# Prefetched residual, a pinned first stage and later cache copies in a two-layer hybrid decoder

## The chip, the cores and the metric

The kernel runs on 1 core of one Trainium2 chip. The metric is device time in microseconds (us), the median over runs. PE is TensorE, DVE VectorE, ACT ScalarE, POOL GpSimd; SP, ACT and POOL also issue DMAs, each in a queue of its own.

## The reference

Two decoder layers, in fp32, for 1024 prompt tokens and 8 sample tokens that share the weights. Each sub-layer is wrapped in two RMS norms: h = h + post_norm(f(pre_norm(h))).

```
ap = rms_norm(hp, norm_mix_pre[l]);  a_s = rms_norm(hs, norm_mix_pre[l])
layer 0: q, k, v, r, z = split(x @ w_in)        # 512, 512, 1024, 1024, 16 columns
         log_a = log_sigmoid(z @ w_gate2 + b_gate) / 16
         o, s  = gated linear recurrence over q, k, v, log_a     # 4 heads
         m     = (rms_norm(o, g_head) * silu(r)) @ w_out
layer 1: sliding-window attention (window 128, sinks, partial rotary), samples on a cache
h = h + rms_norm(m, norm_mix_post[l])
h = h + rms_norm(relu(rms_norm(h, norm_ffn_pre[l]) @ w_up[l])**2 @ w_down[l], norm_ffn_post[l])
```

The outputs are both hidden states, the recurrence's states, and the last keys and values. For the samples the key and value cache goes out shifted by one position: 127 old rows per sample are copied, one new row is added.

## The kernel before, in words

**Groups and products.** Group A holds tokens 0 to 511 and the 8 samples (520 columns, in chunks of 256 and 264), group B tokens 512 to 1023. Activations lie with the features on the partitions, in 8 pieces (k) of 128. Each fp32 operand is split into a high part (an ACT copy to fp32r) and a low part (a DVE subtraction), and a product is three matmuls: high by high, low by high, high by low (`mms`, lines 225, 227, 229). A weight tile of 512 rows by 128 columns is fetched on SP's queue (`fetch_w`, line 195, three buffers) and split by ACT and DVE (`split_w`, lines 201 and 202, four buffers). The 16 gate columns z have their own `fetch_z`, `split_z` (lines 236, 241, 242) and `mms_z` (line 260).

**Order.** A scheduler may reorder instructions on each engine; those handed to `tc.keep_in_program_order` keep their order among themselves. Products stand in a list (`pending`), and work beside them is written as generators that `tick` advances: each step yields an estimate of its time, and each product gives credit.

**First stage.** `load_x` reads A's tokens in blocks of 128 (`fetch`, line 457) and the gain vector, spread over 128 partitions (line 496). For each block `stats` squares it with a row sum on ACT (line 465), makes the mean on DVE (468) and the -0.5 power on POOL (469); `scale` multiplies two halves by it and by the gain on DVE (477); `turn` transposes on PE (489) and splits into xh and xl (304, 305). Blocks go in the order 0, 1, 2, 3, samples; SP fetches block 0, gain, blocks 1 and 2, wz and two weight tiles, block 3, samples. The splits of wz and of the weights of the first tile of r come behind the squares of block 2, those of the second tile behind block 3. `gla_part1` then runs for A, chunk by chunk, z and the first two tiles of r, and calls `load_params` (lines 131 to 143: eleven small loads on POOL, line 117, with nine DVE operations behind them). `load_gate` (six loads on POOL, line 444, then lines 445 and 446) comes behind A's blocks. The samples' part of the cache copies (line 1098, DRAM to DRAM, on POOL) stands in the second layer's code; nothing holds it there.

**Residual.** `post_norm` scales piece k by gain and rstd (line 371) and calls `residual(k)`. After the first layer's mixer that is `from_input`: ACT's queue fetches the piece's columns of x (line 387, three buffers shared with the norms), PE turns four blocks (391), DVE adds (393); for A a 4 KB load of the samples' columns (396), a transpose (398) and an addition (399) follow, for each piece. The next norm (`pre_norm`, through `rstd_gen`) squares each piece on ACT (317, 320), adds the squares on DVE (321), and makes the new xh and xl (361, 304, 305). This runs beside group B's output projection; A's FFN comes next on PE.

Of the kernel before, what the change touches and what calls it, by code (L numbers as in the profile page):

```python
# [12 lines left out]
F32 = mybir.dt.float32  # L13
# [55 lines left out]
def tile_hybrid_gla_swa_decoder(  # L69
# [50 lines left out]
    def halved(t, n, name):  # L120

        o = const.tile([P, n], F32, name=name)
        nc.vector.tensor_scalar_mul(o, t, -0.5)
        return o
# [6 lines left out]
    def load_params():  # L131
        nonlocal bg_t, gh_t, bqkv_t, bo_t, bq8
        bg_t = load_cols(b_gate[0], GH, "bg_t")
        gh_t = halved(load_cols(g_head[0], 2, "gh_r"), 2, "gh_t")
# [7 lines left out]
        bq8 = const.tile([P, 8], F32, name="bq8")  # L142
        nc.vector.tensor_scalar_mul(bq8, bqkv_t[:, 0:8], 0.125)
# [297 lines left out]
    def load_gate():  # L441
# [3 lines left out]
        nc.scalar.copy(out=wg3, in_=wgs)  # L445
        nc.vector.tensor_tensor(out=wg3[64:96], in0=wgs[64:96], in1=r(wg3[64:96]), op=ALU.subtract)

    def load_x(g, box, tiles, early=None):
# [3 lines left out]
        blocks = list(range(g.nb)) + ([g.nb] if g.ns else [])  # L452

        def fetch(n):
            rows = P if n < g.nb else g.ns
            src = x_prompt[0, (g.b0 + n) * P:(g.b0 + n + 1) * P, :] if n < g.nb else x_sample[:, 0, :]
            nc.sync.dma_start(out=tiles[n][:rows], in_=src)

        def stats(n):
# [5 lines left out]
            sq = nc.scalar.activation(out=jk[:rows], in_=t, func=AF.Square, accum_out=ss[:rows, 0:1])  # L465
            if g.i == 0 and n > 0:
                tc.keep_in_program_order(sq)
            nc.vector.tensor_scalar(out=ms, in0=ss[:rows, 0:1], scalar1=1.0 / D, scalar2=EPS, op0=ALU.mult, op1=ALU.add)
            nc.gpsimd.tensor_tensor(out=y, in0=ms, in1=half[:rows], op=ALU.pow)
            return y  # L470

        def scale(n, y, pin=False):
            rows = P if n < g.nb else g.ns
            t = tiles[n][:rows]
            for hf in range(2):
                c = slice(hf * 512, hf * 512 + 512)
                v = nc.vector.scalar_tensor_tensor(out=t[:, c], in0=t[:, c], scalar=y, in1=gbc[:rows, c],
                                                   op0=ALU.mult, op1=ALU.mult)
                if pin:
                    tc.keep_in_program_order(v)  # L480

        def turn(n):
            rows = P if n < g.nb else g.ns
            t = tiles[n][:rows]
            for hf in range(2):
# [12 lines left out]
        if not ahead:  # L498
            for i in range(len(blocks)):
                fetch(blocks[i])  # L500
                scale(blocks[i], stats(blocks[i]))
                yield YD * (2 if i == 0 else 1)
                turn(blocks[i])
                yield YD
            return
        for i in range(len(blocks) + 1):
            if i + 2 < len(blocks):
                fetch(blocks[i + 2])

            last = i == 2  # L510
            if i < len(blocks):
                y = stats(blocks[i])
                if not last:
                    scale(blocks[i], y, i == 3)
            if i in early and not last:
                early[i]()
            if i > 0:
                turn(blocks[i - 1])
                yield YD
            if last:  # L520
                early[i]()
                scale(blocks[i], y, True)

    def gla_part1(g, x, needs, wz=None):
# [34 lines left out]
        else:  # L559
# [520 lines left out]
    def swa_samples(S, sp, g):  # L1080
# [262 lines left out]
    wA = []  # L1343
    tA = Task(load_x(A, xA, [x0[:, n * D:(n + 1) * D] for n in range(4)] + [xtk], {
# [124 lines left out]
```

## Time and profile before

| | |
|---|---|
| runs | 2276.26 us median of 3 (2276.2 to 2276.66) |
| profiled execution | 2277.55 us |
| its span on the core | 2275.7 us |
| PE busy | 2247.7 us, 99% of the span |
| DVE, ACT, POOL busy | 1470.3, 1218.5, 88.7 us |
| idle of PE before line 489, first | 9.9 us |
| wait of line 391 for loads of x | 1.9 us, two times |

Times are from the start of the span. A group is a line of the kernel with its engine and operation. Idle time before an instruction is put down to what released it last. A matmul's end is modelled, so starts and their distances say more than its duration.

### The profile page before, as it was taken

The numbers are of one execution on the slowest core, as the hardware profiler recorded it, in microseconds if no ns is written. First come the engines' busy times: TensorE is split into PE (matmuls) and PEld (weight loads), VectorE is DVE, ScalarE is ACT, GpSimd is POOL, SyncE is SP. The second block draws the span as 40 slices with busy tenths as digits, with TensorE's granted clock in tenths as the row PEclk, the third lists the DMA queues.
The fourth block names the chain that finished last, engine by engine and source line by source line (L and its number), as shares of the span: only waits on it lengthen the run. The fifth ranks groups of instructions, "written<-read, shape, count | busy, mean of one in ns | idle before, by whom it ended". The sixth has DMA issues, their size and how long they took to land.

```text
span 2275.7 us, 39181 instructions
## 1 busy us (share of the span) xinstructions
PE 2247.7 (99%) x14612; PEld 2043.4 (90%) x14612; DVE 1470.3 (65%) x3166; ACT 1218.5 (54%) x2575; POOL 88.7 (4%) x133
## 2 busy tenths in 40 slices
PE   7999999999999999999999999999999999999998
PEld 7998889889999998998888989989999899888886
DVE  5578665676644457666887487658888478544445
ACT  5556644475434445535766456536766456443433
POOL 4010000100000000120000000020000000000000
PEclk9999999999999999999999999999999999999999
DMA  5444322445333335343222354432222354533322
GB/s 169 130 117 118 98 74 77 126 137 157 94 93 90 93 93 170 95 115 88 80 86 78 99 161 135 128 106 85 75 79 76 93 162 127 162 120 93 102 86 77
DMA packets 389183, 247.25 MB, mean 109 GB/s; under 512 B 17816, under 2 KB 368120, under 8 KB 388192
## 3 DMA queue, kind: packets, MB, share of 16 engines
q1 hardware_dynamic: 360736, 196.85, 29.9%
q10 hardware_dynamic: 24000, 25.58, 3.8%
q0 software_dynamic: 4256, 22.31, 2.9%
q8 instruction: 115, 1.88, 0.3%
q14 instruction: 76, 0.62, 0.1%
HBM read 221.19 MB, written 24.25 MB: 108 GB/s over the span
## 4 chain that ended last, share of the span: by engine, by line
PE 92%; DVE 3%; DMA 2%; ACT 1%; issue 1%; ACTq 0%; POOL 0%; DVEq 0%; SPq 0%; POOLq 0%
PE psl L225 25%; PE psl L227 25%; PE psl L229 25%; PE psd L1291 2%; PE psd L1293 2%; PE psd L1292 2%; PE psc L1012 1%; PE ppt L1041 1%; PE pO L727 1%; PE pO L725 1%; PE po L1052 1%; PE po L1053 1%; PE pP L700 1%; DMA wst<-in_swa_w_qkv_dram 0%; DVE wl L202 0%
## 5 line engine op out<-in xcount | busy, mean ns | idle before, releaser
L225 PE MATMUL psl<-xh,wh 128*128 128x512 f32 (+2 forms) x2784 | 890.8, 320 | 0.6 <-ACT sr L554 0.4
L227 PE MATMUL psl<-xl,wh 128*128 128x512 f32 (+2 forms) x2784 | 886.8, 319 | 0.1
L229 PE MATMUL psl<-xh,wl 128*128 128x512 f32 (+2 forms) x2784 | 886.1, 318 | 0.6 <-DVE wl L202 0.5
L201 ACT CAST wh<-wst 128x512 fp32r<-128x512 f32 x656 | 405.4, 620 | 599.6 <-PE psl L227 477.1
L202 DVE TENSOR_TENSOR wl<-wst,wh 128x512 fp32r<-128x512 f32 x656 | 457.8, 700 | 304.1 <-ACT wh L201 282.1
L225 PEld LDWEIGHTS psl<-xh,wh 128*128 128x128 f32 x2784 | 524.2, 188 | 37.1 <-ACT sr L554 0.6
L229 PEld LDWEIGHTS psl<-xh,wl 128*128 128x128 f32 x2784 | 523.6, 188 | 37.5 <-DVE wl L202 1.0
L227 PEld LDWEIGHTS psl<-xl,wh 128*128 128x128 f32 x2784 | 524.2, 188 | 36.4 <-DVE xl L305 0.3
L227 PE MATMUL psl<-hl,wh 128*128 128x256 f32 (+2 forms) x1280 | 390.8, 305 | 0.0
L225 PE MATMUL psl<-hh,wh 128*128 128x256 f32 (+2 forms) x1280 | 390.7, 305 | 0.1
L229 PE MATMUL psl<-hh,wl 128*128 128x256 f32 (+2 forms) x1280 | 390.3, 305 | 0.0
L225 PEld LDWEIGHTS psl<-hh,wh 128*128 128x128 f32 x1280 | 240.9, 188 | 11.3 <-ACT hh L304 0.5
L229 PEld LDWEIGHTS psl<-hh,wl 128*128 128x128 f32 x1280 | 240.9, 188 | 10.7
L227 PEld LDWEIGHTS psl<-hl,wh 128*128 128x128 f32 x1280 | 240.6, 188 | 11.0
L305 DVE TENSOR_TENSOR hl<-rl,hh 128x256 fp32r<-128x256 f32 (+1 forms) x192 | 98.7, 514 | 165.7 <-ACT hh L304 165.1
L836 DVE TENSOR_TENSOR yf<-yf,psl 128x256 f32<-128x256 f32 (+2 forms) x280 | 132.7, 474 | 81.9 <-PE psl L229 79.8
L823 ACT ACTIVATE rl<-psl 128x256 f32<-128x256 f32 (+1 forms) x192 | 87.1, 454 | 93.0 <-PE psl L229 85.2
L1291 PE MATMUL psd<-wls,hh 128*128 128x512 f32 x256 | 101.4, 397 | 0.0
L1293 PE MATMUL psd<-whs,hh 128*128 128x512 f32 x256 | 100.6, 394 | 0.0
L1292 PE MATMUL psd<-wls,hl 128*128 128x512 f32 x256 | 100.5, 393 | 0.0
L824 ACT ACTIVATE rl<-rl 128x256 f32<-128x256 f32 (+1 forms) x192 | 94.5, 492 | 4.5
L304 ACT CAST hh<-rl 128x256 fp32r<-128x256 f32 (+1 forms) x192 | 92.2, 480 | 4.8 <-ACT rl L824 0.7
(327 smaller groups left out, 2348.3 us busy)
## 6 DMA issues: line engine op xcount, KB each, us to landing
wst<-in_ffn_w_up_dram SPq DMA_DIRECT2D x256, 256.0 KB
wst<-in_ffn_w_down_dram SPq DMA_DIRECT2D x256, 256.0 KB
wst<-in_gla_w_in_dram SPq DMA_DIRECT2D x96, 256.0 KB
wst<-in_swa_w_qkv_dram SPq DMA_DIRECT2D x48, 256.0 KB
wst<-in_gla_w_out_dram SPq DMA_DIRECT2D x32, 256.0 KB
wst<-in_swa_w_out_dram SPq DMA_DIRECT2D x32, 256.0 KB
nx<-xs ACTq DMA_DIRECT2D x24, 260.0 KB
xs<-y POOLq DMA_DIRECT2D x2, 2080.0 KB, 8.7
```

The source lines that it names most:

```text
L201: c = nc.scalar.copy(out=wh, in_=st)
L202: s = nc.vector.tensor_tensor(out=wl, in0=st, in1=r(wh), op=ALU.subtract)
L225: nc.tensor.matmul(o, lhsT=wh[:, k % 4, :m], rhs=xh[:, k, c0:c0 + n], start=(k == 0), stop=False)
L227: nc.tensor.matmul(o, lhsT=wh[:, k % 4, :m], rhs=xl[:, k, c0:c0 + n], start=False, stop=False)
L229: nc.tensor.matmul(o, lhsT=wl[:, k % 4, :m], rhs=xh[:, k, c0:c0 + n], start=False, stop=(k == kt - 1))
L304: nc.scalar.copy(out=h, in_=src)
L305: nc.vector.tensor_tensor(out=l, in0=src, in1=r(h), op=ALU.subtract)
L824: nc.scalar.activation(out=rl, in_=rl, func=AF.Square)
L836: nc.vector.tensor_tensor(out=o, in0=o, in1=ps, op=ALU.add)
L1291: nc.tensor.matmul(ps, lhsT=h[:, tok], rhs=wh, start=(k == 0), stop=False)
L1292: nc.tensor.matmul(ps, lhsT=l[:, tok], rhs=wh, start=False, stop=False)
L1293: nc.tensor.matmul(ps, lhsT=h[:, tok], rhs=wl, start=False, stop=(k == HB - 1))
```

## The change

- SP fetches the samples second: block 0, samples, gain, block 1, wz and two weight tiles, blocks 2 and 3. The samples' square, mean, power and scaling come between those of block 0 and block 1.
- Every instruction of A's first stage on ACT, DVE, POOL and PE is pinned in program order, `turn` gives back its DVE subtractions to be placed apart, and B's first block is pinned too. PE gets 20, 6 and 4 transposes of the identity into an unused bank.
- Blocks 2 and 3 are scaled before and turned after the first chunk's z and first tile of r; the second tile's weights are split around them.
- `load_gate` moves behind the second chunk's z, its copies pinned. `load_params` only loads; the DVE operations on the parameters come as a hook behind tile 4 of r. The two cache copies are issued on POOL behind the parameters' loads, pinned.
- `from_input` for A fetches four pieces of x on POOL when the norm begins, into the buffers `eq` and `ek` (two each), and one more with each piece turned; the samples come in one load, eight transposes at k = 5 and one addition at k = 7.

```diff
-                    gains[nm, l] = halved(load_cols(src[l], KT, f"gr_{nm}{l}"), KT, f"g_{nm}{l}")
+                    raw[nm, l] = load_cols(src[l], KT, f"gr_{nm}{l}")
...
+        def rest():
+            nonlocal gh_t, bq8
+            gh_t = halved(gh_r, 2, "gh_t")
+            for (nm, l), t in raw.items():
+                gains[nm, l] = halved(t, KT, f"g_{nm}{l}")
+            bq8 = const.tile([P, 8], F32, name="bq8")
+            tc.keep_in_program_order(nc.vector.tensor_scalar_mul(bq8, bqkv_t[:, 0:8], 0.125))
+        return rest
...
+        ahead, xm, ps = [], None, None
+
+        def load_ahead():
+            xt = gp.tile([P, NMAX], F32, tag=("eq", "ek")[len(ahead) % 2], name="nxe", bufs=2)
+            ahead.append(load(len(ahead), nc.gpsimd, xt[:, :TB].rearrange("p (n d) -> p n d", d=P)))
+
+        if g.ns:
+            for _ in range(4):
+                load_ahead()
+            xm = gp.tile([P, D], F32, tag="Sp", name="xsm", bufs=1)[:NS]
+            nc.gpsimd.dma_start(out=xm, in_=x_sample[:, 0, :])
+
         def add_x(k):
-            xt = npool.tile([P, 4, P], F32, tag="nt", name="nxi", bufs=3)
-            nc.scalar.dma_start(out=xt, in_=x_prompt[0, g.b0 * P:(g.b0 + 4) * P, k * P:(k + 1) * P].rearrange(
-                "(n p) d -> p n d", p=P))
+            nonlocal ps
+            if g.ns:
+                xt = ahead[k]
+            else:
+                xt = load(k, nc.scalar, npool.tile([P, 4, P], F32, tag="nt", name="nxi", bufs=3))
...
             if g.ns:
-                xm = npool.tile([NS, P], F32, tag="xsm", name="xsm", bufs=1)
-                nc.scalar.dma_start(out=xm, in_=x_sample[:, 0, k * P:(k + 1) * P])
-                ps = aux([P, NS], "pxs")
-                nc.tensor.transpose(ps, xm, ident[:NS, :NS])
-                nc.vector.tensor_tensor(out=y[:, k, TB:TB + NS], in0=y[:, k, TB:TB + NS], in1=ps, op=ALU.add)
+                if len(ahead) < KT:
+                    load_ahead()
+                if k == KT - 3:
+                    ps = aux([P, KT, NS], "pxs")
+                    for kk in range(KT):
+                        nc.tensor.transpose(ps[:, kk, :], xm[:, kk * P:(kk + 1) * P], ident[:NS, :NS])
+                if k == KT - 1:
+                    nc.vector.tensor_tensor(out=y[:, :, TB:TB + NS], in0=y[:, :, TB:TB + NS], in1=ps, op=ALU.add)
         return add_x
...
+            square(n, t, jk[:rows], ss[:rows, 0:1])
+            return mean(ms, ss[:rows, 0:1], y)
...
-                    nc.tensor.transpose(pt[:, k, :rows], t[:, kk * P:(kk + 1) * P], ident[:rows, :rows])
-                split(h[:, hf * 4:hf * 4 + 4, n * P:n * P + rows], l[:, hf * 4:hf * 4 + 4, n * P:n * P + rows],
-                      pt[:, :, :rows])
-
-        ahead = 1 if early is not None else 0
-        if ahead:
-            fetch(0)
-            nc.sync.dma_start(out=gbc, in_=n_mix_pre[0:1, :].broadcast_to([P, D]))
-            fetch(1)
-        if not ahead:
+                    pin(nc.tensor.transpose(pt[:, k, :rows], t[:, kk * P:(kk + 1) * P], ident[:rows, :rows]))
+                ks = slice(hf * 4, hf * 4 + 4)
+                cs = slice(n * P, n * P + rows)
+                pin(nc.scalar.copy(out=h[:, ks, cs], in_=pt[:, :, :rows]))
+
+                def f(pt=pt, ks=ks, cs=cs):
+                    pin(nc.vector.tensor_tensor(out=l[:, ks, cs], in0=pt[:, :, :rows], in1=r(h[:, ks, cs]),
+                                                op=ALU.subtract))
+                low.append(f)
+            return low
...
+        def pin(ins):
+
+            if g.i == 0 or first:
+                tc.keep_in_program_order(ins)
+
+        def warm(n):
+
+            for _ in range(n):
+                pin(nc.tensor.transpose(idle[:, :P], ident, ident))
...
+        idle = ps_lin.tile([P, 512], F32, tag="lin", name="idle")
+        fetch(0)
+        fetch(g.nb)
+        nc.sync.dma_start(out=gbc, in_=n_mix_pre[0:1, :].broadcast_to([P, D]))
+        fetch(1)
+        early["fetch"]()
+        fetch(2)
+        fetch(3)
+        warm(20)
+        y0 = stats(0)
+        ys = stats(g.nb)
+        scale(0, y0)
+        scale(g.nb, ys)
+        y1 = stats(1)
+        l0 = turn(0)
+        l0[0]()
+        scale(1, y1)
+        l0[1]()
+        ls = turn(g.nb)
+        warm(6)
+        early["z"]()
+        l1 = turn(1)
+        warm(4)
+        for f in l1:
+            f()
+        early["r"]()
+        early["fetch1"]()
+        y2 = stats(2)
+        scale(2, y2)
+        y3 = stats(3)
+        scale(3, y3)
+        for f in ls:
+            f()
+        early["r1"](3)
+        yield YD
+        l2 = turn(2)
+        for f in l2:
+            f()
+        l3 = turn(3)
+        early["r1"](4)
+        for f in l3:
+            f()
+        yield YD
...
-                mms_z(wz[3], x, [c], ev_z)
-                for t in range(t0):
-                    mms(wz[4 + t], KT, P, x, [c], ev_r(t))
-            load_params()
+                mms_z(wz["z"], x, [c], ev_z)
+                if c is g.chunks[1]:
+                    load_gate()
+                mms(wz["r"], KT, P, x, [c], ev_r(0))
+                if c is g.chunks[0]:
+                    wz["more"]()
+                mms(wz["r1"], KT, P, x, [c], ev_r(1))
+            hooks[4] = load_params()
+            for c, o in ((cache_k, ks_o), (cache_v, vs_o)):
+                tc.keep_in_program_order(
+                    nc.gpsimd.dma_start(out=o[0, :, 0:127].rearrange("b s k d -> b s (k d)"),
+                                        in_=c[0, :, 1:128].rearrange("b s k d -> b s (k d)")))
...
-            nc.gpsimd.dma_start(out=o[0, :, 0:127].rearrange("b s k d -> b s (k d)"),
-                                in_=cache[0, :, 1:128].rearrange("b s k d -> b s (k d)"))
...
+    early = {"fetch": lambda: st.extend([fetch_z(w_in[0], 3072)] + [fetch_w(w_in[0], k, 2048) for k in (0, 512)]),
+             "z": lambda: wA.update(z=split_z(st[0], True)),
+             "r": lambda: wA.update(r=split_r(1)),
+             "fetch1": lambda: st.extend([fetch_w(w_in[0], k, 2048 + P) for k in (0, 512)]),
+             "r1": lambda i: wA.setdefault("r1", []).append(split_w(st[i], True))}
+    gA = load_x(A, xA, [x0[:, n * D:(n + 1) * D] for n in range(4)] + [xtk], early)
+    next(gA)
+    wA["more"] = lambda: next(gA)
```

## Rows read from the trace of the kernel before

**Rows 1.** The profile's page, first part: busy us, share of the span, instructions.

```profile
PE 2247.7 (99%) x14612; PEld 2043.4 (90%) x14612; DVE 1470.3 (65%) x3166; ACT 1218.5 (54%) x2575; POOL 88.7 (4%) x133
```

**Rows 2.** Busy time by stretch: its length, PE, PEld, DVE, ACT, POOL, PEclk, DMA share, GB/s.

```profile
9.94:13.62 3.68, 3.67 (x16) 3.27 (x16) 3.23 (x6) 2.26 (x5) 1.10 (x6) 1.00 1.07 362
13.62:15.63 2.01, 0.00 (x1) 0.01 (x1) 1.69 (x5) 2.01 (x5) 0.57 (x1) 1.00 0.60 259
15.63:25.10 9.47, 9.47 (x80) 9.02 (x80) 8.04 (x15) 6.46 (x14) 3.01 (x5) 1.00 0.64 207
25.10:27.60 2.50, 1.45 (x14) 1.18 (x14) 1.57 (x5) 0.74 (x3) 2.50 (x6) 1.00 0.68 183
27.60:31.10 3.50, 3.50 (x19) 2.77 (x17) 0.14 (x1) 0.64 (x2) 2.86 (x5) 0.51 0.69 194
31.10:54.90 23.80, 23.80 (x200) 23.71 (x199) 14.81 (x37) 14.23 (x30) 7.33 (x9) 1.00 0.43 91
...
443.20:446.10 2.90, 0.98 (x7) 0.58 (x6) 2.42 (x5) 1.08 (x2) 0.00 (x0) 1.00 0.88 262
...
484.00:2261.00 1777.00, 1775.25 (x11485) 1617.27 (x11484) 1142.61 (x2510) 949.83 (x2064) 40.57 (x39) 1.00 0.36 107
```

**Rows 3.** Line 489 in 0 to 14 us and 20 to 23: ns min/median/max, starts.

```profile
L489 PE MATMUL xT<-ident,x x16: 421/421/473, 9.9 to 13.2; 128*128 128x128 f32 x16
...
L489 PE MATMUL xT<-ident,x x16: 272/273/273, 20.6 to 22.2; 128*128 128x128 f32 x16
```

**Rows 4.** Timeline of DVE, 0 to 62 us: start us, us, line, operation, count, [idle before <-releaser].

```profile
9.01 0.15 DVE L468 TENSOR_SCALAR xss<-xss 128x1 f32<-128x1 f32 x1 [3.19 <-ACT xsq L465]
9.13 2.74 DVE L477 SCALAR_TENSOR_TENSOR x<-x,xss,scr 128x512 f32<-128x512 f32 x4
...
15.29 0.28 DVE L242 TENSOR_TENSOR wz<-wst,wz 128x128 fp32r<-128x128 f32 x1
...
21.85 1.29 DVE L305 TENSOR_TENSOR xl<-xT,xh 128x512 fp32r<-128x512 f32 x2
...
25.04 1.39 DVE L477 SCALAR_TENSOR_TENSOR scr<-scr,xss 8x512 f32<-8x512 f32 x2
```

**Rows 5.** Timeline of ACT, 0 to 62 us.

```profile
4.49 1.06 ACT L465 ACTIVATE xsq<-x 128x1024 f32<-128x1024 f32 x1 [2.16 <-DMA x<-in_x_prompt_dram]
...
7.83 1.06 ACT L465 ACTIVATE xsq<-x 128x1024 f32<-128x1024 f32 x1 [2.19 <-DMA x<-in_x_prompt_dram]
```

**Rows 6.** Timeline of SP's queue, 0 to 62 us.

```profile
9.11 0.38 SPq L457 DMA_DIRECT2D scr<-in_x_sample_dram  x1
```

**Rows 7.** Timeline of POOL, 0 to 62 us.

```profile
5.90 0.57 POOL L469 TENSOR_TENSOR xss<-xss,half 128x1 f32<-128x1 f32 x1 [0.41 <-DVE xss L468]
...
10.40 0.65 POOL L1098 DMA_DIRECT2D out_dram<-in_cache_swa_k_dram  x1
```

**Rows 8.** Timeline of PE, 443 to 490 us.

```profile
444.08 0.63 PE L391 MATMUL pxi<-ident,nxi 128*128 128x128 f32 x4 [0.71 <-DMA nxi<-in_x_prompt_dram]
...
446.07 0.66 PE L391 MATMUL pxi<-ident,nxi 128*128 128x128 f32 x4 [1.21 <-DMA nxi<-in_x_prompt_dram]
```

**Rows 9.** The chain of waits, 438 to 450 us: start us, us, what.

```profile
442.02 4.00 DMA nxi<-in_x_prompt_dram
```

**Rows 10.** Timeline of DVE, 436 to 492 us.

```profile
444.87 0.68 DVE L393 TENSOR_TENSOR y<-y,pxi 128x512 f32<-128x512 f32 x1
...
447.37 1.42 DVE L371 SCALAR_TENSOR_TENSOR y<-y,g_mpost,nrs 128x520 f32<-128x520 f32 x2
...
466.18 1.50 DVE L321 TENSOR_TENSOR nacc<-nacc,nsq 128x520 f32<-128x520 f32 x2
...
484.85 0.68 DVE L202 TENSOR_TENSOR wl<-wst,wh 128x512 fp32r<-128x512 f32 x1
```

**Rows 11.** DMA issues: KB each, median us from issue to landing.

```profile
gain<-in_norm_ffn_post_dram POOLq DMA_DIRECT2D x2, 256.0 KB, 4.1
```

**Rows 12.** Line 320 in 440 to 470 us: ns min/median/max.

```profile
L320 ACT ACTIVATE nsq<-y x7: 623/638/640, 458.3 to 466.3; 128x520 f32<-128x520 f32 x7
```

More of the change, by code (lines that the diff above doesn't have):

```diff
@@ L122, in halved @@
         o = const.tile([P, n], F32, name=name)
-        nc.vector.tensor_scalar_mul(o, t, -0.5)
+        tc.keep_in_program_order(nc.vector.tensor_scalar_mul(o, t, -0.5))
         return o
@@ L133, in load_params @@
         bg_t = load_cols(b_gate[0], GH, "bg_t")
-        gh_t = halved(load_cols(g_head[0], 2, "gh_r"), 2, "gh_t")
+        gh_r = load_cols(g_head[0], 2, "gh_r")
+        raw = {}
         for l in range(2):
@@ L444, in load_gate @@
             tc.keep_in_program_order(nc.gpsimd.dma_start(out=wgs[i * RANK:(i + 1) * RANK, :], in_=w_gate2[0]))
-        nc.scalar.copy(out=wg3, in_=wgs)
-        nc.vector.tensor_tensor(out=wg3[64:96], in0=wgs[64:96], in1=r(wg3[64:96]), op=ALU.subtract)
+        tc.keep_in_program_order(nc.scalar.copy(out=wg3, in_=wgs))
+        tc.keep_in_program_order(
+            nc.vector.tensor_tensor(out=wg3[64:96], in0=wgs[64:96], in1=r(wg3[64:96]), op=ALU.subtract))
     def load_x(g, box, tiles, early=None):
@@ L452, in load_x @@
         blocks = list(range(g.nb)) + ([g.nb] if g.ns else [])
+        first = False
         def fetch(n):
@@ L456, in fetch @@
             src = x_prompt[0, (g.b0 + n) * P:(g.b0 + n + 1) * P, :] if n < g.nb else x_sample[:, 0, :]
-            nc.sync.dma_start(out=tiles[n][:rows], in_=src)
+            return nc.sync.dma_start(out=tiles[n][:rows], in_=src)
         def stats(n):
@@ L464, in stats, with square, mean, scale @@
             ms, y = ss[:rows, 1:2], ss[:rows, 2:3]
[L465 to L469, printed above, removed]
+            square(n, t, jk[:rows], ss[:rows, 0:1])
+            return mean(ms, ss[:rows, 0:1], y)
+        def square(n, t, jk, s):
+            pin(nc.scalar.activation(out=jk, in_=t, func=AF.Square, accum_out=s))
+        def mean(ms, s, y):
+            pin(nc.vector.tensor_scalar(out=ms, in0=s, scalar1=1.0 / D, scalar2=EPS, op0=ALU.mult, op1=ALU.add))
+            pin(nc.gpsimd.tensor_tensor(out=y, in0=ms, in1=half[:y.shape[0]], op=ALU.pow))
             return y
-        def scale(n, y, pin=False):
+        def scale(n, y, hfs=(0, 1)):
             rows = P if n < g.nb else g.ns
             t = tiles[n][:rows]
-            for hf in range(2):
+            for hf in hfs:
                 c = slice(hf * 512, hf * 512 + 512)
[L477 to L482, printed above, removed]
+                pin(nc.vector.scalar_tensor_tensor(out=t[:, c], in0=t[:, c], scalar=y, in1=gbc[:rows, c],
+                                                   op0=ALU.mult, op1=ALU.mult))
+        def turn(n, hfs=(0, 1)):
             rows = P if n < g.nb else g.ns
             t = tiles[n][:rows]
-            for hf in range(2):
+            low = []
+            for hf in hfs:
                 pt = aux([P, 4, P], "xT")
@@ L502, in load_x @@
+        def warm(n):
+            for _ in range(n):
+                pin(nc.tensor.transpose(idle[:, :P], ident, ident))
+        if early is None:
+            for i in range(len(blocks)):
+                first = i == 0
+                d = fetch(blocks[i])
+                if first:
+                    pin(d)
+                y = stats(blocks[i])
+                first = False
+                scale(blocks[i], y)
                 yield YD * (2 if i == 0 else 1)
-                turn(blocks[i])
+                for f in turn(blocks[i]):
+                    f()
@@ L504, in load_x @@
                 yield YD
             return
[L506 to L522, printed above, removed]
+        idle = ps_lin.tile([P, 512], F32, tag="lin", name="idle")
@@ L524, in gla_part1 @@
+        warm(4)
[17 more added lines that the diff above has]
+        for f in l3:
+            f()
+        yield YD
     def gla_part1(g, x, needs, wz=None):
@@ L1342, in tile_hybrid_gla_swa_decoder, with split_r @@
     x0 = new_big(A, "x0").rearrange("p k n -> p (k n)")
-    wA = []
-    tA = Task(load_x(A, xA, [x0[:, n * D:(n + 1) * D] for n in range(4)] + [xtk], {
-        0: lambda: wA.extend([fetch_z(w_in[0], 3072)] + [fetch_w(w_in[0], k, 2048) for k in (0, 512)]),
-        2: lambda: wA.extend([split_z(wA[0], True), [split_w(st, True) for st in wA[1:3]]]),
-        3: lambda: wA.append([split_w(fetch_w(w_in[0], k, 2048 + P), True) for k in (0, 512)])}), 1)
-    need(tA)
-    load_gate()
+    wA, st = {}, []
+    def split_r(i):
+        return [split_w(t, True) for t in st[i:i + 2]]
+    early = {"fetch": lambda: st.extend([fetch_z(w_in[0], 3072)] + [fetch_w(w_in[0], k, 2048) for k in (0, 512)]),
[6 more added lines that the diff above has]
+    wA["more"] = lambda: next(gA)
     tB = add(load_x(B, xB, [xtk] * 4), SLB)
-    for g, box, ts in ((A, xA, [tA]), (B, xB, [tB])):
+    for g, box, ts in ((A, xA, []), (B, xB, [tB])):
         x = (lambda box=box: box[-1])
```

9 lines of the change are left out of this document (5 added, 4 removed).

## The prediction

> **What bounds the kernel now.** I read the page's busy times first, then a table of PE's busy time by stretch, then the timeline of each engine in the first 30 us, then the same around the residual of group A. PE is busy for 2247.7 of 2275.7 us [rows 1], so the whole kernel can lose only 28 us of idle time, and what PE wastes while it is called busy. The table says where that lies [rows 2]: 9.94 us before PE's first instruction (where its first stretch begins), 2.01 us between the first transposes and the first products, 1.05 us idle in 25.10 to 27.60, 1.92 us in 443.20 to 446.10, and only 1.75 us from 484 to 2261. Two stretches are busy but slow. In 27.60 to 31.10 the granted clock reads 0.51, the lower of the two levels (1.2 instead of 2.4 GHz), so about 3.5 x 0.49 = 1.7 us are lost there. And the first 16 transposes last 421 ns each where the same instruction lasts 273 ns from 20.5 on [rows 3]; they follow each other every 0.21 us and not every 0.11, though the column of the table reads 1.00 for them: they too ran at the lower level. After 31 us PE is fed without a pause worth naming, so a microsecond gained in the start is a microsecond gained in all.
>
> **The start, step by step.** The products of the first chunk (tokens 0 to 255, mms_z) need blocks 0 and 1 scaled, turned and split, and the split wz. Today they begin at 15.63, when DVE has done wz [rows 4]. On the way DVE first waits until 9.01 for the mean of block 1, whose square waited for its load until 7.83 [rows 5], and only then scales block 0, whose square was done by about 5.6 [rows 5]. DVE's row from 9.13 to 11.87 is four scalings on end, 0.68 us from start to start [rows 4].
>
> In the new order the samples' fetch goes second on SP. Its issue costs 0.38 us there [rows 6], so the gain vector, block 1 and the weights go out 0.4 us later, while blocks 2 and 3 go behind the three weight fetches. Block 1 then lands near 8.0 instead of 7.8. Engine by engine, with the durations of [rows 4, 5, 7] and 0.65 us for a subtraction of a split (1.29 for two, [rows 4]):
> - ACT: square of block 0 to 5.64, of the samples 5.7 to 6.85 (8 rows cost the same, 1024 columns), of block 1 from 8.0 to 9.15.
> - DVE and POOL: mean of the samples 6.9 to 7.05; the pow of block 0 is ready at 6.5 [rows 7]. Block 0 scaled 7.1 to 8.45, samples 8.45 to 9.85 (1.39 for two, [rows 4]), mean of block 1 to 9.97, its pow 10.6; meanwhile the subtraction for block 0's first half to 10.65; block 1 scaled to 12.0; second subtraction 12.65; wz 12.95; two subtractions for block 1 to 14.25.
> - PE: the first products start at 13.0, are held at the first xl of block 1 (13.6), and run from there: effectively 13.6 instead of 15.63, **2.0 us** earlier.
>
> Behind it DVE remains the slowest: two weight subtractions (to 15.5), the scalings of blocks 2 and 3 with a POOL round trip each (to 19.8), the samples' and z's small subtractions, two weight subtractions and four for blocks 2 and 3, end near 24.5. PE, with 9.47 us of work between the first products and the second chunk's [rows 2], would want that at 13.6 + 9.47 = 23.1; it waits about 1.3 us for DVE in between and begins the second chunk's mms_z at 24.4. Today it lies between 25.10 and 31.10, with the samples' transposes and PE's pauses before it, the last 3.5 us at the lower clock [rows 2]. At full rate its 1.9 us and the 0.5 us of products behind it that today also end by 31.10 would end at 24.4 + 2.4 = 26.8. Gain 31.1 - 26.8 = 4.3 us; 5.6 if DVE never holds PE; 2.6 if a stretch at the lower clock like that of 27.60 comes again in it (1.7). If the samples' rows land as late as block 1 (7.8), DVE's chain begins 2.1 us later and 2.2 are left. I take **4.0**, near the sum of the rows, a little shaded for waits that no row of today's order can show.
>
> The 30 warming transposes lie in PE's idle time: 20 x 0.21 = 4.2 us from about 1.5, over before 7.8; the 6 and the 4 take 1.3 and 0.9 us at the lower clock, in the holes before block 1 is scaled (11.3) and before 13.6. They cost nothing while those holes exist, and at most 2.2 us if the scalings came earlier. Their gain is bounded by [rows 3]: 16 x 0.10 = 1.7 us if the turning of blocks 0 and 1 were on PE's account; it is mostly on DVE's, so I put it at nothing.
>
> **The cache copies** (two of 1016 KB, the first issued at 10.40 today, [rows 7]) leave the first stage and come behind the eleven parameter loads on POOL, near 32 us, in a stretch whose DMA share is 0.43 today [rows 2]. The gate's six loads are issued behind block 3's pow, from about 18.5, and ACT's pinned copy of them waits until about 26; what is queued behind it on ACT are evacuations, and three PSUM buffers cover a microsecond or two. The halved parameters move behind the job of t = 4, off a DVE that has time there. All of these at 0, with 1 us for what is late next.
>
> **Group A's residual.** Today its pieces are fetched on ACT's queue when the norm reaches them, and the transposes of k = 0 and k = 1 wait 0.71 and 1.21 us for them [rows 8]; one fetch stands with 4.00 us in the chain [rows 9]. PE is in order, so the products queued behind stop too: 1.92 us. With four pieces fetched before the norm starts, into buffers that group B's heads left, both waits go: **1.9 us**. Later pieces are fetched when the piece four earlier is turned. DVE needs about 1.4 us a piece (0.7 for the gain, 0.7 for the addition, [rows 10]), so a fetch has 5.6 us; a 256 KB load on POOL took 4.1 [rows 11]. The price is the order of the samples: today their columns are added piece by piece, so that ACT squares finished pieces beside the loop and the last sum ends 1.5 us after the last addition, at 467.68 [rows 10]. Now the columns of all pieces are added at k = 7, and the eight squares (0.64 each, [rows 12]) with their seven additions all come behind it, some 6.3 us. That is 4.7 us more, paid from a loop that should end earlier: eight pieces at 1.4 plus five weight subtractions at 0.7 are 15 us, not the 23 from 442.86 to 466.1. So the chain should end some 3 us sooner and PE only 1.9. The margin is needed, since today DVE's work for the FFN ends just in time: its wl of 484.85 [rows 10] is on the chain, and PE is idle for 0.08 us before it.
>
> **Sum.** 4.0 + 1.9 = 5.9 us. The profiled execution took 2277.55 us (1.85 outside its span), 1.29 above the median of 2276.26; 2277.55 - 5.9 = 2271.65, by the same offset a median of **2270.4**.
>
> **The rivals.** 0.2% is 4.55 us, about what a measurement can tell.
> - *The lower clock comes back.* In 25.10 to 27.60 pauses of 1.05 us among tiny transposes were followed by 3.5 us at the lower level [rows 2]. In the new order PE works about half of 8 to 13.6. If the first products start slow, DVE's slack takes up most; if it falls around the second chunk, 1.7 us go: 2.3 + 1.9, **2272.1**. The same time if the samples land late. Chance 0.16. The Trainium skill (TensorE: Matmul & The Clock Gate, the part on the HAM clock gate) says that the throttled state is the default and that activity lifts it; [rows 2, 3] agree, and by that rule the pauses at 8 to 13.6 speak for this rival.
> - *The squares behind k = 7 bind.* If the loop keeps today's pace, only the 1.9 us of waits gone, DVE ends 4.7 - 1.9 = 2.8 us later and PE stands before the FFN of A: -4.0 + 2.8, **2275.1**. Chance 0.14.
> - *POOL's fetches stall the loop: slower.* Pieces 4 to 7 would each wait for a freed buffer and a slow landing in POOL's queue. At 4.0 us of landing and 1.4 of work each [rows 9, 10], behind four quick pieces (442.9 + 4 x 1.4 = 448.5), the loop ends at 448.5 + 4 x 5.4 = 470.1, the sums 6.3 later at 476.4, 8.7 us late: -4.0 + 8.7, **2281**. On today's clock the gain of the start is used up when the loop ends at 465.4, and the kernel is slower by 0.2% from 470 on. Against it: four buffers ahead. Chance 0.08. The Trainium skill (DMA: Bandwidth & Descriptors, Specifications and Issuing engine by pattern) would put a plain load on the sync queue and gives POOL's path a later first byte, 1 us against 0.6: an estimate from the page of 4 x 0.4 = 1.6 us more in this rival. [rows 9, 11] show 4.00 against 4.1, no such gap at this size.
> - *Nothing gained*, the start's lead being lost to a wait further on, such as the weights' fetches beside the cache copies: **2276**. Chance 0.04.
>
> The forecast has 0.58, own range 2267.8 (5.6 + 1.9 gained, and 1 for what moves behind it) to 2271.7. Faster: 0.58 and a quarter of the first rival, 0.62. Same: the rest of it, the second and the fourth, 0.30. Slower 0.08. The range goes from there to 2276.1, the second rival's time with the same 1 us, which takes in the fourth; the slower one and the tails are left out.
>
> **What would show it.** First products at 13.6, second chunk's near 24.4, a clock of 1.00 from there; no wait of pxi for a load; the sums of the norm ended by 460. If PE idles more than 1 us before 484, the squares were the price; if the first products start after 15, the samples' place was wrong.

## The result, and the profile after

The changed kernel takes **2303.2 us** (median of 4 runs, 2299.3 to 2303.87), against 2276.45 for the kernel before on the same chip: a ratio of 1.011, 95% interval 1.0098 to 1.0122. It is slower by 1.1% where 0.26% faster was forecast, and far outside the range. The profiled execution took 2299.3 us with a span of 2297.5, which is 21.8 over the span of before. What follows is read from that profile; why the median of the 4 runs lies 3.9 us above it is not explained.

The first part of the page, busy us and instructions of each engine, the line that answers to [rows 1]:

```profile
PE 2257.7 (98%) x14642; PEld 2054.6 (89%) x14642; DVE 1468.6 (64%) x3159; ACT 1220.0 (53%) x2575; POOL 95.2 (4%) x142
```

PE is *more* busy than before (2257.7 against 2247.7 us). Its 30 more matmuls are the warming transposes, and these make 6.6 of the 10.0 us (3.96, 1.54 and 1.06); they lie in the first 15 us and are not the loss. Where the loss lies, the table of PE by stretch tells. Columns as in [rows 2]: length, PE, PEld, DVE, ACT, POOL, PEclk, DMA share, GB/s.

```profile
10.00:13.00 3.00, 3.00 (x18) 2.98 (x19) 2.68 (x6) 1.32 (x5) 0.56 (x1) 0.50 0.86 327
13.00:14.00 1.00, 1.00 (x7) 1.00 (x6) 0.30 (x3) 0.59 (x1) 0.00 (x0) 0.50 0.02 8
14.00:15.00 1.00, 1.00 (x7) 0.90 (x6) 0.84 (x2) 0.86 (x2) 0.00 (x0) 0.53 0.49 119
15.00:16.00 1.00, 1.00 (x10) 0.88 (x9) 1.00 (x3) 1.00 (x3) 0.00 (x0) 1.00 0.48 143
...
100.00:120.00 20.00, 6.40 (x36) 5.45 (x34) 7.39 (x13) 5.61 (x10) 1.10 (x2) 0.68 0.23 72
120.00:140.00 20.00, 13.24 (x90) 12.99 (x91) 16.08 (x33) 13.31 (x25) 1.07 (x4) 0.73 0.14 41
...
465.40:468.30 2.90, 2.90 (x22) 2.67 (x21) 2.90 (x6) 1.11 (x2) 1.95 (x3) 1.00 0.46 126
...
500.00:510.00 10.00, 7.76 (x40) 7.05 (x39) 9.31 (x15) 6.63 (x12) 0.00 (x0) 0.83 0.32 91
```

The two lines from 100 to 140 us hold the loss: PE works 19.6 of 40 us, and at granted clocks of 0.68 and 0.73. Before, PE was busy for all of these 40 us, at 1.00. Idle 20.4 us, and at the lower clock 6.40 x 0.32 + 13.24 x 0.27 = 5.6 us: some 26 lost. By PE's products it is 24: the kernel is ahead by 1.9 us near 32 us and behind by 22.2 near 437, as is shown further below. Both stretches named by the prediction are in the table too. The stretch of 443.20 to 446.10 lies 22.2 us later now, at 465.40 to 468.30, and is full (2.90 of 2.90); 10 to 14 runs at 0.50.

What PE waits for, from the groups of waits (us in total, times, longest):

```profile
PE xT L526 <- DVE scr L514: 20.4, 3, 7.2
...
PE psl L237 <- DVE wl L210: 2.5, 2, 2.2
```

The turning of group B's four token blocks waits three times for DVE's scaling, 20.4 us in all. Before there was no such wait. The chain of waits shows how it goes (start, us, what; short pieces left out):

```profile
101.15 0.89 PE xT L526 x8
102.06 3.31 DMA scr<-in_x_prompt_dram
...
105.48 1.16 ACT xsq L502 x2
106.66 0.17 DVE xss L505
...
106.96 0.56 POOL xss L506
...
107.54 0.76 DVE scr L514
...
108.35 1.98 PE xT L526 x8
...
110.78 3.76 DMA scr<-in_x_prompt_dram
```

Each block runs alone through fetch (3.3 to 3.8 us), square (1.16), mean (0.17), power (0.56), scaling (0.76 for the first half) and turning (1.98). All four blocks pass through one buffer (`xtk`), so the next fetch starts only when the block before is turned: SP's queue stands there for 17.83 us, and the weights' loads stand behind it on that queue.

```profile
102.06 17.83 SPq L490 DMA_DIRECT2D scr<-in_x_prompt_dram  x3
```

Why are the four blocks so late and so close together? Not because anything was slow. POOL's timeline has the two cache copies and B's powers:

```profile
32.28 0.59 POOL L657 DMA_DIRECT2D out_dram<-in_cache_swa_k_dram  x1
32.87 0.57 POOL L657 DMA_DIRECT2D out_dram<-in_cache_swa_v_dram  x1
38.23 0.56 POOL L506 TENSOR_TENSOR xss<-xss,half 128x1 f32<-128x1 f32 x1 [4.79 <-DVE xss L505]
...
106.96 0.55 POOL L506 TENSOR_TENSOR xss<-xss,half 128x1 f32<-128x1 f32 x1 [25.21 <-DVE xss L505]
```

The copies took 0.59 and 0.57 us of POOL, at 32.28 as the prediction said, they had landed by 42.5, and the power of B's first block followed at 38.23, against 37.34 in the kernel before. But DVE scaled that block 61 us later, without waiting for anything (the row has no releaser):

```profile
99.48 1.41 DVE L514 SCALAR_TENSOR_TENSOR scr<-scr,xss 128x512 f32<-128x512 f32 x2
...
107.54 1.41 DVE L514 SCALAR_TENSOR_TENSOR scr<-scr,xss 128x512 f32<-128x512 f32 x2 [0.73 <-POOL xss L506]
```

That is because its place in DVE's order is late. The orders of the compiled kernels show this without a run; a row is a group of like instructions on end. On PE, B's four turnings stand at rows 181, 326, 423 and 570 of the order before, and from row 688 on, nearly on end, after the change. On POOL, the change puts the copies straight in front of B's first power:

```
before                                   after
25 DMA cache k (line 1098)               26 POW x3
26 POW x2                                27 DMA wgs x6
27 DMA cache v                           28 to 38 the parameters
28 POW (samples)                         39 DMA cache k (line 657)
29 DMA wgs x6                            40 DMA cache v
30 to 40 the parameters                  41 POW (B's first block)
41 POW x3 (B's first three blocks)       44 POW x2
43 POW (B's last)                        46 POW
```

So my first theory, called C in what follows: the scheduler, which fixes each engine's order beforehand, reckons the copies (two of 1016 KB) as long work of POOL. B's powers come late in its reckoning, so it puts all that hangs on them late. The chip finds the copies done in 0.6 us each, but must keep the order.

### The profile page after: what moved, and what is told of

The parts are those of the page before. It is cut to its first block, busy times and chain, and to the rows that moved or that the text cites. A ratio compares the mean times of both kernels' runs of the same rounds, so it can differ in the third digit from the quotient of the medians.

```text
span 2297.5 us, 39225 instructions
## 1 busy us (share of the span) xinstructions
PE 2257.7 (98%) x14642; PEld 2054.6 (89%) x14642; DVE 1468.6 (64%) x3159; ACT 1220.0 (53%) x2575; POOL 95.2 (4%) x142
## 4 chain that ended last, share of the span: by engine, by line
PE 93%; DVE 3%; ACT 1%; DMA 1%; issue 1%; POOL 0%; DVEq 0%; ACTq 0%; POOLq 0%
PE psl L233 26%; PE psl L235 26%; PE psl L237 26%; PE psd L1379 2%; PE psd L1381 2%; PE psd L1380 2%; PE psc L1102 1%; PE ppt L1131 1%; PE pO L817 1%; PE pO L815 1%; PE po L1142 1%; PE po L1143 1%; PE xT L526 1%; PE pP L790 1%; DMA wst<-in_gla_w_out_dram 0%
```

## The experiments

Each ratio is to the kernel before on the same chip, with its 95% interval.

**Which part costs the 27 us.** Three kernels: the changed one with the copies where they were, the kernel before with nothing but the copies moved, and the changed one with B's first block unpinned.

The changed kernel with the copies back (the kernel before with the copies moved is the same edit the other way round):

```diff
-            for c, o in ((cache_k, ks_o), (cache_v, vs_o)):
-                tc.keep_in_program_order(
-                    nc.gpsimd.dma_start(out=o[0, :, 0:127].rearrange("b s k d -> b s (k d)"),
-                                        in_=c[0, :, 1:128].rearrange("b s k d -> b s (k d)")))
...
         for t, o, cache in ((ksm, ks_o, cache_k), (g.vsm, vs_o, cache_v)):
+            nc.gpsimd.dma_start(out=o[0, :, 0:127].rearrange("b s k d -> b s (k d)"),
+                                in_=cache[0, :, 1:128].rearrange("b s k d -> b s (k d)"))
```

and in `pin` of the third:

```diff
-            if g.i == 0 or first:
+            if g.i == 0:
```

> Only the two cache copies go back to their old place; the pinned first stage, the warming, the parameters' hook and A's prefetched residual stay. Theory C (the order is planned ahead, and the copies in front of group B's power on POOL push B's four token blocks to the end of the plan, where PE stands for them): the blocks spread out again, no wait of the transposes of B for their scaling between 95 and 130 us, about 24 us less than the changed kernel, 2277 to 2281. Rival P (the pinning itself, of A's first stage and of B's first block, does that): still 2295 or more.

> The kernel before with this one edit: the copies pinned behind the eleven parameter loads. Theory C: B's blocks come late and in one heap, 20 us of waits for their scaling, 2297 to 2301. Rival P: no change, 2276.

> The changed kernel without the pinning of group B's first block (the copies stay where the change put them). Theory C: no help, because the power of B's first block still has nothing but the copies in front of it, 2299 to 2304. Rival P: 2277 to 2281.

Measured: copies back 2277.49, ratio 0.9997 (0.9987 to 1.0007). Only the copies moved 2300.79, 1.0105 (1.009 to 1.012). B's block unpinned 2299.12, 1.0094 (1.0074 to 1.0115). The moved copies alone reproduce the whole loss, in a kernel whose first stage and residual are the old ones, and with the same wait:

```profile
PE xT L489 <- DVE scr L477: 19.8, 3, 6.8
```

The pin on B's first block has no part in it.

**Copies elsewhere.** The changed kernel with the copies pinned in the second layer's code, behind all of B's powers:

```diff
         for t, o, cache in ((ksm, ks_o, cache_k), (g.vsm, vs_o, cache_v)):
+            tc.keep_in_program_order(
+                nc.gpsimd.dma_start(out=o[0, :, 0:127].rearrange("b s k d -> b s (k d)"),
+                                    in_=cache[0, :, 1:128].rearrange("b s k d -> b s (k d)")))
```

> The changed kernel with the copies pinned where the second layer's code has them, so behind all powers of B on POOL. Theory C: 2275 to 2280, and up to 2 us less than with the copies at their old place, since they no longer run beside the loads of the first stage. Rival P: 2295 or more. If the residual of A costs what it seems to (3.3 us of idle time and some at the lower clock from 500 to 512), both this and the run with the copies back stay above the kernel before or beside it.

Measured: 2282.54, ratio 1.0022 (1.0012 to 1.0031), above the 2275 to 2280 expected. B's blocks are spread out again. At PE's sums of A's first norm, near 437 us, this kernel leads by 2.8 us. One copy now lies at 469.3 and one at 1001.2. The lead is still 2.0 near 913 and is lost by 1303: in between, the waits of PE for the attention's probabilities (ppt for pb) grew from 0.4 to 3.4 us.

**Is it POOL, or the traffic?** Same place in the program, another queue:

```diff
-                    nc.gpsimd.dma_start(out=o[0, :, 0:127].rearrange("b s k d -> b s (k d)"),
+                    nc.scalar.dma_start(out=o[0, :, 0:127].rearrange("b s k d -> b s (k d)"),
```

> The changed kernel with one word altered: the two cache copies are issued at the very same place in the program, behind the parameters, but on ACT's queue and not on POOL's. Theory C (the plan reckons the copies as long work of POOL, puts group B's powers behind them and so B's scaling and turning at the end): B's blocks come spread out again, no transposes wait 6 to 7 us for DVE, and some 24 us come back: 2276 to 2279. Rival (the traffic of the copies at that place, or their place in the program whatever the queue): B's blocks stay late, 2295 or more.

Measured: 2277.32, ratio 1.0001 (0.9992 to 1.001). The traffic is the same and is issued at the same place of the program, 3 to 4 us later on the chip (35.54 and 36.90), but the loss is gone. DVE scales B's blocks spread out (the fourth follows at 79.71):

```profile
39.78 1.42 DVE L514 SCALAR_TENSOR_TENSOR scr<-scr,xss 128x512 f32<-128x512 f32 x2 [0.75 <-POOL xss L506]
...
53.83 1.41 DVE L514 SCALAR_TENSOR_TENSOR scr<-scr,xss 128x512 f32<-128x512 f32 x2 [0.73 <-POOL xss L506]
...
67.16 1.42 DVE L514 SCALAR_TENSOR_TENSOR scr<-scr,xss 128x512 f32<-128x512 f32 x2 [0.73 <-POOL xss L506]
```

That settles the cause as far as these runs can: two copies pinned in *POOL's* order straight in front of B's powers. To stand ahead of these powers is not enough: in the kernel before the copies do so too, unpinned and earlier (10.40 and 18.05 us), and B's blocks come in time. No run separates the pin from the place. That the scheduler prices the copies as long is the reading that fits, but its prices are not in any trace.

**What the rest of the change is worth.** With copies back, the first stage and the residual together gained nothing, not the 5.9 us forecast. Four kernels ask where it went. Start only is the kernel with copies back and the old `from_input`; residual only is the kernel before with the new `from_input`. The third adds to residual only this edit of `norms`:

```diff
-        nc.gpsimd.dma_start(out=xs[g.i], in_=y)
         h, l = new_xn(g)
         box.append((h, l))
         yield from pre_norm(y, g, gpre, h, l, halve)
+        nc.gpsimd.dma_start(out=xs[g.i], in_=y)
```

and the fourth is start only with the copies pinned in `load_x` right behind the power of B's last block:

```diff
                 y = stats(blocks[i])
+                if i == len(blocks) - 1:
+                    for c, o in ((cache_k, ks_o), (cache_v, vs_o)):
+                        tc.keep_in_program_order(
+                            nc.gpsimd.dma_start(out=o[0, :, 0:127].rearrange("b s k d -> b s (k d)"),
+                                                in_=c[0, :, 1:128].rearrange("b s k d -> b s (k d)")))
```

> The changed kernel with the cache copies at their old place and the old residual: of the change only the first stage is left. In the run with copies back and the new residual, r's copy of the second chunk stood at 33.83 us (34.15 before) and the time was 2277.5, the same as before. Theory R (the new residual wins 1.9 us at the transposes and gives them back before the feed-forward of A, where PE stood 2.6 us in 480 to 485 and then ran at a granted clock of 0.68): this run keeps only the 0.3 us of the start, 2277.0, and PE is idle near 443 to 446 by 1.9 us as before and not in 480 to 485. Rival S (the start is worth the predicted 4 us and the new residual costs that much): 2273.4.

> The kernel before with only the new residual. Theory R: PE's 1.9 us near 443 to 446 are gone, and about as much is idle or slow between 480 and 490, behind weight subtractions whose loads came late beside the 2 MB write of y and the loads of the second layer's constants on POOL: 2277 within 1. Rival S, if the new residual costs as much as the start was to win: 2281. If the prediction's step was right as it stands and the two parts only disturb each other: 2275.4.

> The run before this one (new residual alone) with one line moved: the 2 MB write of y to DRAM is issued behind the norm's last column block instead of ahead of its squares. Theory R, crowd part (the loads of the last weights of the output projection are late because they share the DMA engines with that write): ACT's wait of 4.6 us for wst near 470 goes, PE's idle time in 480 to 490 falls below 1 us and the time to 2275.4, 1.9 under the run with the new residual alone. Rival (DVE's own work bounds the feed-forward's start, whatever the loads do): no more than 0.5 us apart.

> The new first stage with the old residual, and the two cache copies pinned right behind the power of group B's last block on POOL, so that they are neither beside the first loads nor ahead of B's powers. Theory C says that B's four blocks are turned spread out as before, with no wait of 6 to 7 us of the transposes. The start then keeps what it showed with the copies out of it (r's copy of the second chunk at 32.3 instead of 34.15 us): 1.9 us under before, 2275.4. If the start were worth the predicted 4 us: 2273.3. If the copies disturb whatever stands behind them: 2280 or more.

Measured: start only 2278.94, 1.0006 (0.9998 to 1.0015), some 2 us over the 2277.0 of R and 5.5 over S: the start's lead of 0.9 us at 437 was gone at the old residual, where the clock fell to 0.76 in 443 to 450. Residual only 2277.06, 0.9999 (0.999 to 1.0008). Write's line moved 2276.92, 0.9999 (0.999 to 1.0007). Copies behind B's last power 2284.21, 1.003 (1.0019 to 1.0041), a miss for every time but the last, though B's blocks came spread out as C says: PE idled 3.5 us in 140 to 200 (0.9 before) and 2.2 in 900 to 1100 (0.3 before), and I did not follow that up.

For the residual the chain of the run with it alone names the price:

```profile
461.90 10.49 DMA wst<-in_gla_w_out_dram
472.48 0.63 ACT wh L201
473.13 0.69 DVE wl L202
473.82 2.01 DVE nxn L361 x3
...
484.68 0.61 DVE wl L202
485.33 0.39 PE psl L229
```

Theory R, in the expectations above, says that the residual gives back in the feed-forward what it wins at the transposes. The load of the last weights of the output projection took 10.49 us, ACT's wh waited for it, then DVE's wl, and behind that wl on DVE stood the norm's scalings (nxn), which could have gone 3.6 us sooner. So PE, which gained 1.92 us at the transposes, waited 2.87 us for DVE at 485.33. Beside that load lies the 2 MB write of y (xs), issued at 461.55; the DMA share is 0.79 in 460 to 465 and 0.97 in 465 to 470. The mask's and the sinks' loads are there too, at 459.95 to 465.5; before they went at about 430 to 436. The run with the write's line moved tested nothing: unpinned, the write left POOL at 465.97 amid the sinks, and the load took 10.45 us. So the write has to be pinned.

**The write pinned behind the norm**, first for every norm (in residual only, and in the changed kernel with the copies on ACT's queue), then only where `residual is from_input and g.ns`, which is A's first norm (in the changed kernel with the copies on ACT's queue):

```diff
-        nc.gpsimd.dma_start(out=xs[g.i], in_=y)
...
         yield from pre_norm(y, g, gpre, h, l, halve)
+        tc.keep_in_program_order(nc.scalar.dma_start(out=xs[g.i], in_=y))
```

> The kernel before with the new residual, and the 2 MB write of y (of every norm) issued from ACT's queue and pinned behind the norm's last block; in the run that only moved its line it left POOL at 465.97, amid the loads of the sinks, as ever, and decided nothing. Theory R, crowd part: the fetch of the last weights of the output projection, 10.5 us in the chain of the run with the new residual alone, falls below 6 us, DVE's wait of 3.6 us for ACT's wh goes, PE's idle time in 480 to 490 falls under 1 us, and the time to 2274 to 2275.5, some 2 us under before. Rival (DVE's own work or the loads of the sinks): PE idle there 2 us or more, 2277 within 0.7.

> Both edits in the changed kernel: copies on ACT's queue, and the write of y pinned behind the norm's last block on ACT's queue. If C and R hold, the parts add up: 1.9 us of the start and 1.9 us of the residual under before, 2273, and this version beats both kernels. If R falls: 2275 to 2278, as the run with the copies on ACT's queue alone.

> The changed kernel with the copies on ACT's queue, and only the first norm of A's write of y issued from ACT's queue and pinned behind its last block; the other norms' writes stay on POOL, where pinning all of them cost 2.4, 0.5 and 1.4 us of idle PE in three later stretches of the run before. Theory R, crowd part: of PE's 2.44 us of idle time in 480 to 485 in the run with the copies on ACT's queue about 1.2 remain, a little later, beside the write, the clock stays at 1.00 around it, and later stretches idle as in that run: 2275 to 2276, 1.2 to 2.4 under it. Rival (any edit makes the plan reorder what follows, and as much is lost elsewhere): 2277.3 or more.

Measured: every norm's write pinned 2280.53, 1.0015 (1.0006 to 1.0024), and in the changed kernel 2279.9, 1.0014 (1.0005 to 1.0023): both above every expectation. ACT's wait for the load is gone in both and PE idles 1.2 and 1.1 us in 480 to 490, but in 913 to 1000, beside a later pinned write at 930, PE idles 2.35 and 3.29 us (0.33 before). Only A's first: **2275.51, ratio 0.9989 (0.998 to 0.9998)**, beside 2277.74 for the kernel before: the one version that beats both kernels, by 0.1%, with an interval that just excludes 1. The table by stretch, 460 to 490 us (columns as above), of the kernel with the copies on ACT's queue alone:

```profile
465.00:470.00 5.00, 5.00 (x23) 4.13 (x22) 2.22 (x6) 0.66 (x3) 1.39 (x3) 1.00 0.96 302
...
480.00:485.00 5.00, 2.56 (x14) 2.41 (x13) 4.95 (x9) 3.94 (x9) 0.00 (x0) 0.79 0.24 66
485.00:490.00 5.00, 5.00 (x39) 5.00 (x38) 4.05 (x7) 3.88 (x9) 0.00 (x0) 0.87 0.50 142
```

and of the one with A's first write pinned behind the norm:

```profile
465.00:470.00 5.00, 5.00 (x24) 4.14 (x23) 4.63 (x11) 2.38 (x6) 1.58 (x4) 1.00 0.55 165
...
480.00:485.00 5.00, 5.00 (x40) 4.84 (x40) 1.26 (x3) 1.83 (x5) 0.00 (x0) 1.00 0.99 326
485.00:490.00 5.00, 3.75 (x29) 3.33 (x28) 4.76 (x9) 5.00 (x12) 0.00 (x0) 1.00 0.39 112
```

The crowd is gone from 465 to 470 (DMA share 0.55 for 0.96), DVE works 4.63 of those 5 us in place of 2.22, and PE idles 1.25 us beside the late write, not 2.44, at a clock of 1.00, not 0.79 and 0.87. These two kernels differ in this one write, so the crowd part of R holds, the write being its main piece.

To see where each kernel gains or loses, here are the starts of the same PE products (a norm's sums) in the profiled runs, as differences to the kernel before, in us; negative is sooner:

| kernel | at 437.28 | at 569.65 | at 1302.75 | span |
|---|---|---|---|---|
| after | +22.2 | +21.7 | +21.7 | +21.8 |
| copies back | 0.0 | -0.2 | -0.1 | +0.1 |
| start only | -0.9 | +1.0 | +2.5 | +2.7 |
| residual only | +0.8 | -0.1 | +0.2 | -0.2 |
| copies late | -2.8 | -2.0 | +4.3 | +4.3 |
| copies behind B's last power | +2.5 | +1.5 | +5.1 | +6.6 |
| copies on ACT | -1.0 | -1.3 | +0.1 | +0.6 |
| residual, every write pinned | 0.0 | -2.8 | +0.5 | +2.6 |
| copies on ACT, every write pinned | +1.5 | -1.3 | +4.2 | +5.1 |
| copies on ACT, A's write pinned | 0.0 | -2.8 | -2.1 | -1.8 |

Between 437 and 570 the residual alone gains 0.9, with the write behind the norm 2.8. Single profiles scatter: the kernel with the residual alone has the old first stage and still stands at +0.8 by 437. The three kernels with the copies on ACT have the same first stage and differ by up to 2.5 there.

## Why the prediction was wrong

**The step that failed** is "The cache copies ... All of these at 0, with 1 us for what is late next". It measured +23 us (2300.79 against 2277.35 with the copies alone moved). The copies came behind the eleven parameter loads near 32 us, as it said, and held POOL for only 1.2 us. What was not asked is who stands behind them on POOL. [rows 7] show a power of the first stage; the powers of B's blocks follow the parameters on the same engine, and 61 us of delay came from where the scheduler put their users, not from an engine's time. Working with durations from a trace, the prediction took the order of everything it didn't name as given. The rival "slower" had the wrong mechanism: POOL's fetches for the residual never stalled the loop, so its direction came true by luck. The two gains failed as well: with the copies back, 5.9 us were forecast and 2277.49 against 2277.35 measured. The parts below say which terms were wrong.

**First products at 13.6.** They came at 14.61, 1.0 us sooner than before, not 2.0. PE's timeline of the first stage:

```profile
12.19 1.91 PE L526 MATMUL xT<-ident,x 128*128 128x128 f32 x8
13.89 1.06 PE L545 MATMUL idle<-ident 128*128 128x128 f32 x4
14.61 0.51 PE L268 MATMUL psz<-xh,wz 128*32 128x256 f32 x1
...
24.07 0.31 PE L268 MATMUL psz<-xh,wz 128*32 128x264 f32 x1 [0.50 <-ACT xh L529]
...
25.07 0.38 PE L233 MATMUL psl<-xh,wh 128*128 128x256 f32 x1 [0.57 <-ACT wh L209]
...
27.08 0.28 PE L268 MATMUL psz<-xl,wz 128*16 128x264 f32 x1
```

and DVE's:

```profile
12.92 0.28 DVE L250 TENSOR_TENSOR wz<-wst,wz 128x128 fp32r<-128x128 f32 x1
13.90 0.69 DVE L532 TENSOR_TENSOR xl<-xT,xh 128x512 fp32r<-128x512 f32 x1 [0.70 <-ACT xh L529]
```

DVE kept to the forecast within 0.3 us up to wz (its end at 13.20, forecast 12.95). The missing microsecond is block 1's turning, 1.91 us for 8 transposes at the lower clock, behind six warming transposes: the first subtraction for block 1 could start only at 13.90, where the forecast had 12.95. Block 1's first half was scaled by about 11.7 and PE began to turn it at 12.19, so by these rows the pinned warming itself holds about half of that microsecond. "They cost nothing" was wrong, and "I put it at nothing" was the wrong price for that clock; with this order the turning is on the path. The 20 transposes from 1.47 to 5.43 did not keep the clock up: PE then idled 2.61 us, and the table has 0.50, the level of 1.2 GHz, in 10 to 14. It has 1.00 from 15 on, after PE had worked without a pause since 8.04. The rule of the Trainium skill that the forecast quoted (TensorE: Matmul & The Clock Gate, the part on the HAM clock gate) says that activity lifts the clock; the rise near 15 agrees, but it came too late for the turning.

**Second chunk near 24.4.** Its first product came at 24.07, but that was one product. PE then waited for ACT's wh and DVE's wl of the first chunk's second tile of r (0.57 and 0.22 in the same timeline) and went on with the chunk at 27.08, where before it did at 27.23. What was won behind it is the lower clock, which before lay at 27.60 to 31.10 [rows 2] and now is 1.00: ACT's first copy of r for the second chunk is at 32.26, before at 34.15. So the term measured **1.9, not 4.0**, under every case of the sum (2.2 to 5.6). With the cache copies back beside the first loads it is 0.3 (33.83), and by 437 us between 0 and 1 us is left with the copies back (0.0 and, with the old residual, 0.9). The rival of the lower clock had the right resource in the wrong place.

**The residual.** No transpose waits for a load, the 1.92 us are won, and DVE's last addition of the squares ends 24.6 us after PE's products that open the norm (484.1 after 459.5), before 30.4 (467.7 after 437.3): 5.8 us sooner, where 3 were forecast. The squares did not bind: the rival "the squares behind k = 7" falls. The sign set for it did show, more than 1 us of idle PE before the feed-forward (2.64 us in 480 to 485 with the copies back), but from another cause. What the step lacked is what a sooner end *triggers*: the write of y went out while the last weights were still being fetched. The chain of waits of the changed kernel, 480 to 506 us, shows the same load as the run with the residual alone, 9.88 us long:

```profile
482.76 9.88 DMA wst<-in_gla_w_out_dram
...
492.72 0.63 ACT wh L209
...
493.37 0.69 DVE wl L210
494.07 2.01 DVE nxn L369 x3
...
504.91 0.61 DVE wl L210
...
505.57 0.38 PE psl L237
```

Behind it PE waited 2.24 us (its longest for wl is in the groups of waits above), and the clock was 0.83 around it. "So the chain should end some 3 us sooner and PE only 1.9" took DVE to be the only thing in the way. The margin it counted was eaten by one DMA. POOL's fetches landed no later than ACT's: 4.1 us in the median of eight (3.2 to 5.2) against 4.00 in [rows 9]. The Trainium skill (DMA: Bandwidth & Descriptors, Specifications) gives POOL's path a later first byte; at this size the runs show no such gap.

**Open.** Five kernels with the new first stage and B's blocks in their old places lost 1.4 to 6.3 us between 913 and 1303 us (copies late, start only, copies behind B's last power, copies on ACT with and without every write pinned). The first stage alone is not the reason: the kernels with the copies back or with A's write pinned have it too and lose 0.1 and 0.7 there, and residual only with every write pinned, which has the old one, loses 2.6. The start-only kernel, for one, has this wait there, where the kernel before waits 0.2 us:

```profile
PE psl L233 <- ACT xh L312: 1.9, 1, 1.9
```

Nothing of the change lies there except one copy in one kernel and the pinned writes in another. That the scheduler orders the second layer anew after each edit would explain it; no run shows it. The first stage without its ten later warming transposes wasn't tried.

## What to carry to other kernels

When an instruction is moved, list what follows it in the program on the same engine and compare the compiled orders before any timing: B's turnings had gone from row 181 to row 688, and that was nearly the whole result. Two transfers whose issue took 0.6 us each cost 23 here, by the order that the scheduler made around them; a queue on which nothing urgent hangs cost nothing (2277.32 against 2277.49). And when a chain is made to end sooner, ask what its end sets off, and what that meets.

## What the runs showed of the hardware

- A 256 KB weight load took 10.49 us in the chain of the kernel with the new residual alone, beside a 2 MB write and some small loads (DMA share 0.79 and 0.97); the residual's fetches of the same size took 4.1 in the changed kernel.
- Two DRAM to DRAM copies of 1016 KB held POOL for 0.59 and 0.57 us.
- Three of B's blocks, each turned after a wait of PE of 6.3 to 7.2 us, took 1.98 us each, and 1.04 in the kernel before, where PE had no such wait; the granted clock was 0.68 in 100 to 120 us, where the kernel before has 1.00. So beside the idle time these waits came with work at the lower clock.
